# A hybrid decoder layer: a bank of its own for norms, other positions of the mixer's stages, and weight tiles made ahead

## The chip, the cores and the metric

The kernel runs on one NeuronCore of a Trainium2 chip. TensorE (PE) multiplies, and loads its weights in instructions of their own (PEld). VectorE (DVE), ScalarE (ACT) and GpSimd (POOL) do the elementwise work. The queue of SyncE (SP) issues nearly all transfers between DRAM and the on-chip memory. Results of matmuls go to PSUM, eight banks of 512 float32 columns on each of 128 partitions. The metric is the time of the whole program on the device in microseconds; the median of several runs counts.

## The reference

One layer on 512 frames, with 16 meta tokens put ahead of them (528 rows in the kernel, since the pad rows are never computed), model width 1024, all in float32:

```python
h = h + 0.5 * swiglu(rmsnorm(h, norm_ffn1[l]), ffn1_w_in[l], ffn1_w_out[l])
u = rmsnorm(h, norm_mix[l]) * valid
P = u @ w_in[l]
q, kq, vq, rw, gates = jnp.split(P, cols, axis=-1)
...
att = sliding_window_attention(q, kq, vq, sinks[l])
rw = token_shift_lerp(rw, rwkv_mu[l])
r_, k_, v_, wd, ad, gd = jnp.split(rw, rcols, axis=-1)
rwo = rwkv7_time_mix(r_, k_, v_, wd, ad, gd, ...)
g_att, g_rwkv = jnp.split(gates, 2, axis=-1)
merged = (jax.nn.sigmoid(g_att) * (att @ w_attn_branch[l])
          + jax.nn.sigmoid(g_rwkv) * (rwo @ w_rwkv_branch[l]))
h = h + merged @ w_out[l]
h = h + 0.5 * swiglu(rmsnorm(h, norm_ffn2[l]), ffn2_w_in[l], ffn2_w_out[l])
return rmsnorm(h, norm_final)[:, BLOCK:]
```

`swiglu` is `(silu(gate) * up) @ w_out` with 2816 hidden columns. `rwkv7_time_mix` carries a 64 x 64 state for each of 16 heads over all frames: `S = S * w + (S a) b + v k`, `y = S r`.

## The kernel before

**Layout.** Activations lie transposed, eight blocks of 128 features by 528 tokens. Every large product runs in three passes (`products`, L140): each operand is split in a rounded part and the rest (`uh`/`ul`, `whi`/`wlo`), and hi x hi, hi x lo and lo x hi are summed in PSUM. A weight tile of 128 output columns comes in two halves of four feature blocks (256 KB each). `load_w` (L122) loads a half on SyncE's queue into `raw` (three buffers), casts it on ScalarE to `whi` and subtracts on VectorE to get `wlo` (four buffers each).

**Order.** A tile framework puts the instructions in order for every engine by a priority, which is the order in which the program text emits them, and by when it reckons their inputs to be ready. It also sets all waits, among them those on a buffer that is used again. The order on each engine is fixed when the program is built.

**FFN1** (`ffn`, L243). For each of 22 hidden blocks j, the gate's products (`dense`, L258) and then the up products (L261) go to two pairs of banks out of three. The norm is applied behind the product: `nm.end` (L267) sums the squares over features on TensorE (`inverse`, L210), takes the inverse root on VectorE (`rsqrt`) and spreads it over the partitions (L223) into `rstd`; all this uses one bank `pn`. For j = 0 the squares of the first four blocks are made and added on GpSimd (L189 to L194), those of the other four on ScalarE and VectorE. Ahead of it h is loaded in eight pieces, with the four half tiles of j = 0 (both of the gate, both of up) behind pieces 1 and 5. Then eight output blocks, each with its residual addition (L281), its part of the next norm (`tile`, L177) and a store of h.

**Between FFN1 and mixer** (L1089) a new bank `pn` serves `nm.end`, and `scaled` (L226) makes the normalised operand of the mixer. The mixer then takes all eight banks: `dn` 2, `s` 2, `att`, `t`, `y` and `small` 1 each. Its first products, `loras` (L432), and those of `qkv` use the operand that isn't normalised and apply `rstd` later.

**The mixer** (`mixer`, L337) is a set of generators that each `yield` after a step. For each of eight pairs of heads j five stages follow each other: `stage_a1` (projections of k, r, v, the decay, the key norm), `stage_p` (products within chunks of 64 frames, L750), `stage_i` (inverse of the triangular blocks, L839), `stage_b` (the recurrence over nine chunks, L896), `stage_t` (group norm and gate). Beside them run `qkv`, `attend` in eight blocks, 16 `gates` and, at the end, `att_branch`, `reload`, `rwkv_branch`.

`stage_p` clears and fills the blocks `g1` (L767), a ring of two buffers, which `stage_b` reads to its end (L910), and writes the triangular blocks to DRAM (`Ls`, L806). `stage_i` loads them in three copies to `LT` (L847), one buffer, runs 31 steps of a multiplication and an addition on VectorE (L852, L854), writes `Xs` (L858), reads it back to `xt` (L863), and joins the blocks in `assemble` (L870), which uses `LT` as its work space. `stage_b` multiplies by `xt` (L918).

**The planner.** `PLAN` (L40) gives each stage its first position relative to its pair and its span, both in units of one pair; `STEPS` is the number of steps; `SHIFT` moves single stages; `ATTS` and `GATE` are the distances of the attention blocks and gates. `run` (L1002) always emits the step with the lowest position among the stages whose predecessors are done. `LATE` is added to the priority while a step is emitted: a positive number puts its instructions behind others that were emitted later, a negative one ahead.

Of the kernel before, what the change touches and what calls it, by code (L numbers as in the profile page):

```python
# [8 lines left out]
F32 = mybir.dt.float32  # L9
# [30 lines left out]
PLAN = {"qkv": (-3.307, 1), "stage_a1": (-2.9, 1.03), "stage_p": (-1.46, 0.7), "stage_i": (-0.78, 0.75), "stage_b": (-0.201, 0.732),  # L40
        "stage_t": (1.256, 0.532), "att": (-0.985, 0.923), "gate": (-0.058, 1.022), "att_branch": (4.378, 2.027), "reload": (6.272, 0.409), "rwkv_branch": (7.996, 0.282)}
# [57 lines left out]
def hybrid_layer(ctx: ExitStack, tc: tile.TileContext, a, phases="all"):  # L99
# [35 lines left out]
    ready = []  # L135

    def preload(src):
        ready.extend(load_w(src[:, k:k + KW, :], KW) for k in range(0, KD, KW))
# [26 lines left out]
    class Norm:  # L165
# [20 lines left out]
        def square(self, k, h, pool=False):  # L186
            n = self.n
            acc = self.rstd
            if pool:  # L189
                sq = self.tmp.tile([P, NT], F32, name="rms_sq", tag="t")[:, :n] if k else acc[:, :n]  # L190
                nc.gpsimd.tensor_mul(out=sq, in0=h, in1=h)
                if k:
                    nc.gpsimd.tensor_add(out=acc[:, :n], in0=acc[:, :n], in1=sq)
                return  # L194
            if k == 0:
                nc.scalar.activation(out=acc[:, :n], in_=h, func=AF.Square)
            else:
                sq = self.tmp.tile([P, NT], F32, name="rms_sq", tag="t")[:, :n]
                nc.scalar.activation(out=sq, in_=h, func=AF.Square)
                nc.vector.tensor_add(out=acc[:, :n], in0=acc[:, :n], in1=sq)  # L200

        def inverse(self, bank, cols, extra=None):

            n = cols.stop - cols.start
            nb = -(-n // P)
            pt = bank()
            for i, x in enumerate((self.rstd[:, cols], extra)):
                for b in range(nb if x is not None else 0):
                    s0 = min(P * b, n - P)
                    nc.tensor.matmul(pt[:, nb * i + b:nb * i + b + 1], x[:, s0:s0 + P], mean, start=True, stop=True)  # L210
            if extra is None:
                return rsqrt(self.tmp, pt[:, :nb], nb, RMS_EPS)
            ms = self.tmp.tile([P, 8], F32, name="ms")[:, :nb]
            nc.vector.tensor_copy(out=ms, in_=pt[:, :nb])
            nc.vector.tensor_add(out=ms, in0=ms, in1=pt[:, nb:2 * nb])
            return rsqrt(self.tmp, ms, nb, RMS_EPS)
# [26 lines left out]
    def ffn(h, n, nm, w_in, w_out, gain, squares=None):  # L243

        with ExitStack() as es:
# [3 lines left out]
            ps1 = es.enter_context(tc.tile_pool(name="ffn_ps1", bufs=1, space=PSUM))  # L249
            bank = lambda: ps1.tile([P, 512], F32, name="pn")  # L250
# [4 lines left out]
            for j in range(KF):  # L255
                pg = ps2.tile([P, 2, 512], F32, name="dn")
                og, cuts, vg = outs_of(pg, n)
                dense(og, w_in[j, :, 0], nm.uh, nm.ul, KD, cuts)  # L258
                pu = ps2.tile([P, 2, 512], F32, name="dn")
                ou, cuts, vu = outs_of(pu, n)  # L260
                dense(ou, w_in[j, :, 1], nm.uh, nm.ul, KD, cuts)  # L261
# [14 lines left out]
            for i in range(KD - last):  # L276
# [5 lines left out]
                nm.tile(i, h[:, i, :])  # L282
                if gain == "gm":
# [53 lines left out]
    def mixer(nm):  # L337
# [16 lines left out]
        small = ps.tile([P, 512], F32, name="small", bufs=1)  # L354
# [4 lines left out]
        def dense_it(src, cuts, M=P, xh=uh, xl=ul, tags=("dn",), eng=nc.vector):  # L359

            w = []
            for i, c in enumerate(cuts):
                pt = bank(tags[i % len(tags)])[:M, :c.stop - c.start]
                for q in range(KD // KW):
                    if len(w) == q:
                        w.append(load_w(src[:, KW * q:KW * q + KW, :], KW, M, eng))
# [65 lines left out]
        def loras():  # L432
            early = [[x for x in dense_it(w, cuts, M, nm.uh, nm.ul, t) if x[1] is not None]
                     for w, M, cuts, t in ((a["win"][T_LORA], P, HALVES, ("dn",)), (a["win"][T_LORA + 1], P, LATER, ("s",)),
# [32 lines left out]
        def qkv():  # L467
# [6 lines left out]
            for c, pt in dense_it(a["win"][T_VQ], HALVES, P, nm.uh, nm.ul):  # L474
# [592 lines left out]
    with ExitStack() as es:  # L1067
# [21 lines left out]
        with tc.tile_pool(name="nps", bufs=1, space=PSUM) as pn:  # L1089
            nm.tmp = t0  # L1090
            nm.end(lambda: pn.tile([P, 512], F32, name="pn"))
# [3 lines left out]
    with ExitStack() as es:  # L1095
# [110 lines left out]
```

## Time and profile before

| what | us |
|---|---|
| median of 3 runs | 1591.35 |
| lowest, highest run | 1590.21, 1594.18 |
| the profiled execution's own time | 1586.12 |
| its span, first to last instruction | 1584.4 |

By the time line of that execution FFN1 ends at 402.6 us (last product of its last block), the mixer's last result comes at about 1157 us, and the second FFN with its norm fills the rest. Rows of a time line have the start, the time taken, the engine (a q behind it marks the sequencer, which issues and waits), the line of the code, the operation, and the tile that is written and those that are read; xN merges N alike, and in brackets stand the idle time before and what ended it. In a table by stretches each engine has its busy time and its number of instructions. Busy times of PE overlap, as matmuls are pipelined.

### The profile page before, as it was taken

What the parts mean: (1) busy time and instruction counts of PE and PEld (TensorE: products, weight loads), DVE (VectorE), ACT (ScalarE), POOL (GpSimd) and SP (SyncE); (2) the same over time, 40 slices, a digit from 0 to 9 for tenths busy, and PEclk for the clock granted to TensorE, in tenths of its full rate; (3) what the DMA queues carried; (4) which work ended last, traced back from release to release, by engine and by line L of the source; (5) the groups of instructions that cost most, each with busy time, mean ns of one, the idle gap of its engine ahead of it and who ended that gap; (6) DMA issues with size and microseconds to landing.
All of it is one profiled execution on the core that took longest, in us unless ns stands there. A gap on an engine that the chain in (4) does not pass through costs nothing.

```text
span 1584.4 us, 25643 instructions
## 1 busy us (share of the span) xinstructions
PE 1502.9 (95%) x9351; PEld 1322.8 (83%) x9351; DVE 908.3 (57%) x2472; ACT 651.8 (41%) x1464; POOL 103.9 (7%) x159
## 2 busy tenths in 40 slices
PE   7999999999898999999889999979999999999997
PEld 7999999999786887787768788757877888888886
DVE  7434344333745875888888789657555444443334
ACT  4333333232433446474556655644333333333221
POOL 3111111000100100000000000000000011010000
PEclk9999999999899989999999999999999999999998
DMA  5333333333233423133234233347633333333332
GB/s 164 95 89 93 90 91 89 103 110 109 63 111 104 125 72 97 45 96 97 63 102 111 76 96 88 110 147 253 196 104 89 97 94 99 94 98 90 98 91 82
DMA packets 137838, 163.23 MB, mean 103 GB/s; under 512 B 56960, under 2 KB 68288, under 8 KB 137712
## 3 DMA queue, kind: packets, MB, share of 16 engines
q1 hardware_dynamic: 137568, 161.54, 35.0%
q8 instruction: 73, 1.20, 0.3%
q14 instruction: 53, 0.43, 0.1%
q10 hardware_dynamic: 144, 0.06, 0.0%
HBM read 140.03 MB, written 21.52 MB: 102 GB/s over the span
## 4 chain that ended last, share of the span: by engine, by line
PE 77%; DVE 9%; DMA 9%; ACT 3%; issue 2%; SPq 1%; DVEq 0%; ACTq 0%
PE dn L142 17%; PE dn L144 17%; PE dn L143 17%; PE pdn L142 5%; PE pdn L144 4%; PE pdn L143 4%; DMA LT<-Ls 4%; DMA Xs<-X 2%; PE py L923 1%; PE patt L582 1%; DMA raw<-win 1%; PE small L910 1%; DVE wlo L132 1%; PE ps L799 1%; PE small L918 1%
## 5 line engine op out<-in xcount | busy, mean ns | idle before, releaser
L131 ACT CAST whi<-raw 128x512 fp32r<-128x512 f32 (+2 forms) x426 | 259.0, 611 | 594.3 <-PE dn L143 457.7
L132 DVE TENSOR_TENSOR wlo<-raw,whi 128x512 fp32r<-128x512 f32 (+2 forms) x426 | 289.8, 682 | 312.4 <-ACT whi L131 310.9
L142 PE MATMUL dn<-uh,whi 128*128 128x264 f32 (+1 forms) x1320 | 429.5, 326 | 9.1 <-ACT whi L131 6.7
L143 PE MATMUL dn<-ul,whi 128*128 128x264 f32 (+1 forms) x1320 | 427.0, 324 | 1.5 <-DVE ul L181 1.5
L144 PE MATMUL dn<-uh,wlo 128*128 128x264 f32 (+1 forms) x1320 | 427.8, 324 | 0.2 <-DVE wlo L132 0.2
L142 PEld LDWEIGHTS dn<-uh,whi 128*128 128x128 f32 x1320 | 249.5, 189 | 28.8 <-ACT whi L131 9.3
L143 PEld LDWEIGHTS dn<-ul,whi 128*128 128x128 f32 x1320 | 249.8, 189 | 21.9 <-DVE ul L181 2.1
L144 PEld LDWEIGHTS dn<-uh,wlo 128*128 128x128 f32 x1320 | 249.8, 189 | 21.1 <-DVE wlo L132 0.5
L142 PE MATMUL pdn<-uh,whi 128*128 128x264 f32 (+3 forms) x656 | 227.8, 350 | 14.9 <-ACT uh L240 7.4
L144 PE MATMUL pdn<-uh,wlo 128*128 128x264 f32 (+3 forms) x656 | 222.8, 342 | 3.1 <-DVE wlo L132 3.1
L143 PE MATMUL pdn<-ul,whi 128*128 128x264 f32 (+3 forms) x656 | 222.5, 341 | 0.0
L142 PEld LDWEIGHTS pdn<-uh,whi 128*128 128x128 f32 x656 | 127.1, 195 | 29.0 <-ACT uh L240 8.9
L144 PEld LDWEIGHTS pdn<-uh,wlo 128*128 128x128 f32 x656 | 127.1, 194 | 10.7 <-DVE wlo L132 4.6
L143 PEld LDWEIGHTS pdn<-ul,whi 128*128 128x128 f32 x656 | 128.0, 195 | 7.9 <-DVE ul L241 1.5
L143 PE MATMUL dn<-ml,whi 128*128 128x264 f32 (+2 forms) x350 | 110.7, 316 | 0.0
L142 PE MATMUL dn<-mh,whi 128*128 128x264 f32 (+2 forms) x350 | 110.6, 316 | 0.0
L144 PE MATMUL dn<-mh,wlo 128*128 128x264 f32 (+2 forms) x350 | 110.4, 316 | 0.0
L272 POOL TENSOR_TENSOR sg<-sg,rstd 128x528 f32<-128x528 f32 (+1 forms) x44 | 58.0, 1318 | 604.4 <-ACT sg L271 419.0
L273 DVE TENSOR_TENSOR m<-sg,dn 128x528 f32<-128x528 f32 (+1 forms) x44 | 30.6, 696 | 71.0 <-PE dn L144 67.7
L142 PEld LDWEIGHTS dn<-mh,whi 128*128 128x128 f32 x350 | 66.0, 188 | 4.4
L143 PEld LDWEIGHTS dn<-ml,whi 128*128 128x128 f32 x350 | 66.0, 188 | 4.4
L144 PEld LDWEIGHTS dn<-mh,wlo 128*128 128x128 f32 x350 | 66.0, 188 | 4.3
(398 smaller groups left out, 2057.5 us busy)
## 6 DMA issues: line engine op xcount, KB each, us to landing
raw<-win SPq DMA_DIRECT2D x104, 256.0 KB
raw<-w1in SPq DMA_DIRECT2D x88, 256.0 KB
raw<-w2in SPq DMA_DIRECT2D x88, 256.0 KB
raw<-w1out SPq DMA_DIRECT2D x40, 256.0 KB
raw<-w2out SPq DMA_DIRECT2D x40, 256.0 KB
gD<-tgt SPq DMA_DIRECT2D x24, 256.0 KB
raw<-wa SPq DMA_DIRECT2D x16, 256.0 KB
tgt<-gD SPq DMA_DIRECT2D x16, 256.0 KB
```

What stands on the lines that cost most here:

```text
L131: nc.scalar.copy(out=hi, in_=raw)
L132: (eng or nc.vector).tensor_tensor(out=lo, in0=raw, in1=hi.bitcast(F32), op=OP.subtract)
L142: nc.tensor.matmul(o, hi, xh[k][:, c], start=(k == 0), stop=False)
L143: nc.tensor.matmul(o, hi, xl[k][:, c], start=False, stop=False)
L144: nc.tensor.matmul(o, lo, xh[k][:, c], start=False, stop=last)
L272: nc.gpsimd.tensor_mul(out=sg, in0=sg, in1=nm.rstd[:, :n])
L273: nc.vector.tensor_mul(out=vw(m), in0=vw(sg), in1=vu)
L582: nc.tensor.matmul(po[:, x, :], pTs[q][:k1 - k0, P * x:P * x + P], vt[:k1 - k0, q, CH * kv:CH * kv + CH], start=(q == 0), stop=(q == len(p ...
L799: nc.tensor.matmul(pt[:, P * i:P * i + P], KBT[:, c0 + i, :], g1[:, c0 - 1 + i, :], start=True, stop=True)
L910: nc.tensor.matmul(pz[:, U], G.g1[h][:, c - 1, :] if c else G.g0[:, h, :], W[:, c, h, :], start=True, stop=True)
L918: nc.tensor.matmul(pu, G.xt[:, c, :], zy[:, q % 2], start=True, stop=True)
L923: nc.tensor.matmul(py[:, q, h, :], g3[:, c - 1, h, :] if c else G.g3[:, :P], W[:, c, h, :], start=True, stop=True)
```

## The change

- A pool `sm` holds one PSUM bank for the whole program. It serves the norms of both FFNs and the norm between FFN1 and mixer, and it is the mixer's `small`. The extra pools for `pn` go, and behind the mixer three pairs of banks are used instead of four.
- At the start seven products of zeros are run. The half tiles of j = 0 are loaded in another order (first halves of gate and up behind h's piece 0, second halves behind piece 3), and a new `dense_pair` runs gate and up together, block by block of features.
- All squares are made on ScalarE and added on VectorE. `inverse` sums its two parts in PSUM.
- While FFN1 makes its output blocks 2 to 6, one half weight tile of the mixer each is loaded and split into a pool of its own (`FIRST`: both halves of window tiles 0 and 1, the first of tile 27). `dense_it` takes these when it comes to them.
- `PLAN`, `SHIFT`, `ATTS`, `GATE` and `LATE` have other values.

```diff
-PLAN = {"qkv": (-3.307, 1), "stage_a1": (-2.9, 1.03), "stage_p": (-1.46, 0.7), "stage_i": (-0.78, 0.75), "stage_b": (-0.201, 0.732),
-        "stage_t": (1.256, 0.532), "att": (-0.985, 0.923), "gate": (-0.058, 1.022), "att_branch": (4.378, 2.027), "reload": (6.272, 0.409), "rwkv_branch": (7.996, 0.282)}
+PLAN = {"qkv": (-2.771, 0.729), "stage_a1": (-2.83, 0.789), "stage_p": (-1.171, 0.942), "stage_i": (-2.734, 0.587),
+        "stage_b": (-0.138, 0.693), "stage_t": (1.478, 0.214), "att": (-1.614, 1.044), "gate": (0.091, 0.42),
+        "att_branch": (3.86, 1.399), "reload": (6.425, 0.417), "rwkv_branch": (7.903, 0.124)}
...
-SHIFT = {}
-ATTS = 0.971
-GATE = 0.446
-LATE = {"gate": 695, "att_branch": 1783, "reload": 623, "rwkv_branch": 1701, "stage_a1": -77, "stage_t": -265, "stage_p": -66, "stage_i": -182}
+SHIFT = {("stage_t", 5): -0.415, ("stage_i", 7): 0.482, ("stage_b", 2): 0.071, ("stage_a1", 6): -0.027, ("stage_i", 4): -0.133,
...
+        ("stage_t", 7): -0.124, ("stage_t", 1): -0.07, ("stage_i", 0): 0.174, ("stage_p", 5): -0.03, ("stage_b", 7): -0.047}
+
+FIRST = [(0, 0), (0, 1), (1, 0), (1, 1), (27, 0)]
+ATTS = 0.946
+GATE = 0.462
+LATE = {"gate": 337, "att_branch": 1714, "reload": 1055, "rwkv_branch": 2849, "stage_a1": -79, "stage_t": 196, "stage_p": -207,
+        "stage_i": -1108, "qkv": -36, "att": 209, "stage_b": 148}
...
+    sm = ctx.enter_context(tc.tile_pool(name="sm", bufs=1, space=PSUM))
+    bank = lambda: sm.tile([P, 512], F32, name="pn")
     un = ctx.enter_context(ExitStack())
     up = un.enter_context(tc.tile_pool(name="up", bufs=1))
+    pre = un.enter_context(tc.tile_pool(name="pre", bufs=len(FIRST)))
...
+    def dense_pair(outs, src, xh, xl, cuts):
+
+        for k0 in range(0, KD, KW):
+            w = [ready.pop(0) if ready else load_w(src[:, x, k0:k0 + KW, :], KW) for x in range(2)]
+            for k in range(KW):
+                for (hi, lo), oo in zip(w, outs):
+                    for o, c in zip(oo, cuts):
+                        products(o, hi[:, k, :], lo[:, k, :], xh, xl, c, k0 + k, k0 + k == KD - 1)
...
-                            nm.square(k, h[:, k, :], k < 4)
+                            nm.square(k, h[:, k, :])
...
+                if gain == "gm" and i >= 2 and i - 2 < len(FIRST):
+                    t, q = FIRST[i - 2]
+                    first[t, q] = load_w(a["win"][t][:, KW * q:KW * q + KW, :], KW, pool=pre)
...
-        small = ps.tile([P, 512], F32, name="small", bufs=1)
+        small = sm.tile([P, 512], F32, name="pn")
...
+        with tc.tile_pool(name="wps", bufs=1, space=PSUM) as pw:
+            zero, pz = t0.tile([P, 256], F32, name="zero"), pw.tile([P, 512], F32, name="pw")
+            nc.gpsimd.memset(zero, 0.0)
+            for i in range(7):
+                nc.tensor.matmul(pz[:, :256], zero[:, :P], zero, start=True, stop=True)
         for k in range(KD):
             nc.sync.dma_start(out=h[:, k, :], in_=a["xT"][:, k, :])
-            if k in (1, 5) and phases != "mix":
-                preload(a["w1in"][0, :, k // 5])
+            if k in (0, 3) and phases != "mix":
+                preload(a["w1in"][0], KW * (k // 3))
...
-            ps2 = e2.enter_context(tc.tile_pool(name="br_ps", bufs=4, space=PSUM))
+            ps2 = e2.enter_context(tc.tile_pool(name="br_ps", bufs=3, space=PSUM))
```

Left out are the removed GpSimd branch of `square`, the two halves of `inverse` that become one, and the plumbing of `first` through `dense_it`.

More of the change, by code (lines that the diff above doesn't have):

```diff
@@ L39 @@
 PAUSE = {"sq": 1, "rn": 1, "el": 1, "inv": 1}
-PLAN = {"qkv": (-3.307, 1), "stage_a1": (-2.9, 1.03), "stage_p": (-1.46, 0.7), "stage_i": (-0.78, 0.75), "stage_b": (-0.201, 0.732),
-        "stage_t": (1.256, 0.532), "att": (-0.985, 0.923), "gate": (-0.058, 1.022), "att_branch": (4.378, 2.027), "reload": (6.272, 0.409), "rwkv_branch": (7.996, 0.282)}
+PLAN = {"qkv": (-2.771, 0.729), "stage_a1": (-2.83, 0.789), "stage_p": (-1.171, 0.942), "stage_i": (-2.734, 0.587),
+        "stage_b": (-0.138, 0.693), "stage_t": (1.478, 0.214), "att": (-1.614, 1.044), "gate": (0.091, 0.42),
+        "att_branch": (3.86, 1.399), "reload": (6.425, 0.417), "rwkv_branch": (7.903, 0.124)}
 STEPS = {"qkv": 30, "stage_a1": 19, "stage_p": 13, "stage_i": 9, "stage_b": 27, "stage_t": 5, "att": 13, "gate": 2, "att_branch": 24, "reload": 7,
          "rwkv_branch": 16}
-SHIFT = {}
-ATTS = 0.971
-GATE = 0.446
-LATE = {"gate": 695, "att_branch": 1783, "reload": 623, "rwkv_branch": 1701, "stage_a1": -77, "stage_t": -265, "stage_p": -66, "stage_i": -182}
+SHIFT = {("stage_t", 5): -0.415, ("stage_i", 7): 0.482, ("stage_b", 2): 0.071, ("stage_a1", 6): -0.027, ("stage_i", 4): -0.133,
+        ("stage_t", 2): -0.095, ("stage_b", 3): 0.119, ("stage_p", 1): 0.042, ("stage_t", 4): 0.123, ("stage_t", 3): -0.157,
+        ("stage_t", 0): 0.003, ("stage_i", 6): 0.096, ("stage_p", 2): 0.173, ("stage_i", 3): -0.27, ("stage_i", 2): -0.033,
+        ("stage_a1", 3): 0.319, ("stage_p", 6): 0.183, ("stage_a1", 4): 0.07, ("stage_p", 3): -0.095, ("stage_i", 1): 0.055,
+        ("stage_t", 6): -0.097, ("stage_p", 7): 0.076, ("stage_b", 0): 0.067, ("stage_i", 5): -0.243, ("stage_b", 6): 0.153,
+        ("stage_p", 4): 0.028, ("stage_b", 4): -0.102, ("stage_a1", 0): 0.006, ("stage_a1", 2): 0.186, ("stage_b", 1): -0.009,
+        ("stage_t", 7): -0.124, ("stage_t", 1): -0.07, ("stage_i", 0): 0.174, ("stage_p", 5): -0.03, ("stage_b", 7): -0.047}
[4 more added lines that the diff above has]
+        "stage_i": -1108, "qkv": -36, "att": 209, "stage_b": 148}
 S_DECAY = float(np.exp(np.float32(-0.5)))
@@ L133, in load_w, with preload @@
         return hi, lo
-    ready = []
-    def preload(src):
-        ready.extend(load_w(src[:, k:k + KW, :], KW) for k in range(0, KD, KW))
+    ready, first = [], {}
+    def preload(src, k):
+        ready.extend(load_w(src[:, x, k:k + KW, :], KW) for x in range(2))
     def products(o, hi, lo, xh, xl, c, k, last):
@@ L184, in tile, with square @@
                 self.square(k, h)
-        def square(self, k, h, pool=False):
+        def square(self, k, h):
             n = self.n
             acc = self.rstd
[L189 to L194, printed above, removed]
             if k == 0:
@@ L206, in inverse @@
             pt = bank()
[L207 to L216, printed above, removed]
+            for b in range(nb):
+                s0 = min(P * b, n - P)
+                nc.tensor.matmul(pt[:, b:b + 1], self.rstd[:, cols][:, s0:s0 + P], mean, start=True, stop=extra is None)
+                if extra is not None:
+                    nc.tensor.matmul(pt[:, b:b + 1], extra[:, s0:s0 + P], mean, start=False, stop=True)
+            return rsqrt(self.tmp, pt[:, :nb], nb, RMS_EPS)
         def spread(self, bank, y, n):
@@ L365, in dense_it @@
                     if len(w) == q:
-                        w.append(load_w(src[:, KW * q:KW * q + KW, :], KW, M, eng))
+                        ws = a["win"][src] if isinstance(src, int) else src
+                        x = first.pop((src, q), None) if isinstance(src, int) else None
+                        w.append(x or load_w(ws[:, KW * q:KW * q + KW, :], KW, M, eng))
                     for k in range(KW):
@@ L433, in loras @@
             early = [[x for x in dense_it(w, cuts, M, nm.uh, nm.ul, t) if x[1] is not None]
-                     for w, M, cuts, t in ((a["win"][T_LORA], P, HALVES, ("dn",)), (a["win"][T_LORA + 1], P, LATER, ("s",)),
+                     for w, M, cuts, t in ((T_LORA, P, HALVES, ("dn",)), (T_LORA + 1, P, LATER, ("s",)),
                                            (a["wgd"], 32, LATER, ("att", "y")))]
@@ L473, in qkv @@
             vf = T("E2")
-            for c, pt in dense_it(a["win"][T_VQ], HALVES, P, nm.uh, nm.ul):
+            for c, pt in dense_it(T_VQ, HALVES, P, nm.uh, nm.ul):
                 if pt is None:
@@ L1088, in hybrid_layer @@
             return
-        with tc.tile_pool(name="nps", bufs=1, space=PSUM) as pn:
-            nm.tmp = t0
-            nm.end(lambda: pn.tile([P, 512], F32, name="pn"))
+        nm.tmp = t0
+        nm.end(bank)
         nm.scaled(h)
```

9 lines of the change are left out of this document (5 added, 4 removed).

## The prediction

> **What bounds the kernel now.** I read the page first, then stretches of 40 us, then the mixer's periods, then single instructions in order of time.
>
> ```profile
> span 1584.4 us, 25643 instructions
> PE 1502.9 (95%) x9351; PEld 1322.8 (83%) x9351; DVE 908.3 (57%) x2472; ACT 651.8 (41%) x1464; POOL 103.9 (7%) x159
> PE 77%; DVE 9%; DMA 9%; ACT 3%; issue 2%; SPq 1%; DVEq 0%; ACTq 0%
> ```
> ```profile
> 0.00:40.00 40.00, 30.75 (x212) 29.27 (x213) 27.82 (x44) 19.44 (x31) 13.95 (x15) 1.00 0.53 164
> 40.00:80.00 40.00, 40.00 (x331) 40.00 (x330) 16.82 (x25) 13.17 (x21) 3.97 (x3) 1.00 0.33 93
> ```
> The columns of a stretch are PE, PEld, DVE, ACT and POOL busy with their counts, granted clock, DMA share and GB/s. TensorE carries most of the chain, but a busy PE in the table is not a PE at its rate, so I count matmuls. In the settled first FFN there are 331 in 40 us, 0.121 us each. The first 40 us have 212: (331 - 212) x 0.121 = 14.4 us of TensorE are lost at the start. The other stretches of the FFNs read like the second row but for some 1 us, so what can be won lies at the start, between FFN1 and mixer, and in the mixer.
>
> The mixer is a pipeline of eight head pairs j. Here is one whole period and the sum of the seven from 618 to 1063 us (445 / 7 = 63.6 us each), then the instructions on tile X (the elimination of stage_i, L852 and L854) in the same seven:
>
> ```profile
> 680.00:743.00 63.00, 59.94 (x408) 51.37 (x408) 53.10 (x207) 33.51 (x97) 3.64 (x10) 1.00 0.34 100
> sum 445.00, PE 406.56 PEld 341.13 DVE 352.85 ACT 248.61 POOL 22.16; mean PE 58.08 PEld 48.73 DVE 50.41 ACT 35.52 POOL 3.17
> ```
> ```profile
> sum 445.00, DVE 94.94; mean DVE 13.56
> ```
> No engine is full: VectorE works 50.4 of 63.6 us (79%), weight loads 48.7. So a latency sets the period. The SyncE queue, VectorE, TensorE and GpSimd in order of time show which one, for j = 2:
>
> ```profile
> 668.68 0.39 SPq L806 DMA_DIRECT2D Ls<-gg  x1
> 671.99 0.45 SPq L807 DMA_DIRECT2D Ls<-gg  x1
> 678.26 0.89 SPq L847 DMA_DIRECT2D LT<-Ls  x3
> 725.59 4.23 SPq L858 DMA_DIRECT2D Xs<-X  x3
> 734.05 0.30 SPq L863 DMA_DIRECT2D xt<-Xs  x1
> 741.49 0.91 SPq L847 DMA_DIRECT2D LT<-Ls  x3
> ```
> ```profile
> 688.89 0.19 DVE L852 TENSOR_TENSOR xtmp<-LT,X 102x31 f32<-102x31 f32 x1 [1.21 <-DMA LT<-Ls]
> 725.40 0.16 DVE L854 TENSOR_TENSOR X<-X,xtmp 102x11 f32<-102x11 f32 x1
> ```
> ```profile
> 743.58 0.49 PE L918 MATMUL small<-zy,xt 128*128 128x128 f32 x2 [0.82 <-ACT zy L911]
> 776.13 0.43 PE L910 MATMUL small<-W,g1e 128*128 128x64 f32 x2
> ```
> ```profile
> 654.52 0.95 POOL L767 MEMSET g1e<- 64x1024 f32 x1 [0.65 <-PE small L910]
> 776.69 0.95 POOL L767 MEMSET g1e<- 64x1024 f32 x1 [26.36 <-PE small L910]
> ```
> Read as a loop: LT has one buffer, so its load for j = 3 (741.49) goes out when j = 2 is assembled. From load to load 63.2 us pass: 10.6 until the first elimination step, 36.7 of elimination (688.89 to 725.56), 8.5 until xt is fetched, 7.4 of assembly. The recurrence of stage_b can then go on (743.58). A second loop lies around it: stage_p of pair j clears g1e, a ring of two, when stage_b of pair j - 2 has read it last (654.52, 776.69): 122.2 us for two pairs. In it lie 17.9 us of stage_p until Ls is written, 5.8 of waiting for LT, then the 63.2, then 32.6 of stage_b. Of the 36.7 us of elimination only 13.6 are its own work; in the rest VectorE serves other stages between its 62 dependent steps.
>
> **The change part by part.** *Mixer's positions.* Stage_i is placed at -2.734 instead of -0.78 and its priority goes from -182 to -1108. It cannot come before stage_p of its pair, so all its steps stand directly behind it and ahead of what shares VectorE with it. It moves LT, Xs and xt loads on SyncE, its 62 steps on VectorE, one clear on GpSimd (L860) and the assembly on TensorE and ScalarE past stages a1, b and att. At best the elimination falls from 36.7 to 13.6 us and the 5.8 us of waiting go: the two-pair loop becomes 122.2 - 23.1 - 5.8 = 93.3, or 46.7 a pair. Less than VectorE's own 50.4 is not possible. Against it: stage_p's span grows from 0.70 to 0.942 units, and what yields to stage_i is late instead, the copies of stage_b first. I therefore don't take the floor. The best of the periods above kept VectorE at 53.10 / 63 = 84%; that share for all gives 50.4 / 0.843 = 59.8 us, so 3.8 us x 7 periods = 26.6 us, the term I take. Bounds: full VectorE gives 13.2 x 7 = 92 us; from below there is the loss priced with the rivals. The other stages' shifts have no row of their own and are inside these bounds. Gates and attention end earlier (last gate at 7.44 instead of 7.65, last attention step at 6.05 instead of 6.73), which lets the attention branch fill the time of the last recurrence; I count nothing for it.
>
> *FFN1 to mixer.* TensorE and VectorE there:
>
> ```profile
> 402.32 0.28 PE L144 MATMUL dn<-mh,wlo 128*128 128x264 f32 x1
> 406.19 1.50 PE L210 MATMUL pn<-mean,rstd 128*128 128x1 f32 x10 [3.60 <-DVE rstd L200]
> 410.26 2.05 PE L223 MATMUL pn<-con,ny 128*128 128x128 f32 x8 [2.56 <-DVE ny L320]
> 413.09 0.61 PE L223 MATMUL pn<-con,ny 128*128 128x16 f32 x2 [0.78 <-DVE rstd L237]
> 414.06 0.56 PE L142 MATMUL pdn<-uh,whi 128*128 128x264 f32 x1 [0.36 <-DVE rstd L237]
> 414.63 0.42 PE L144 MATMUL pdn<-uh,wlo 128*128 128x264 f32 x1
> 414.85 0.42 PE L142 MATMUL pdn<-uh,whi 128*128 128x264 f32 x1
> 417.41 0.28 PE L142 MATMUL pdn<-uh,whi 128*128 128x264 f32 x1
> 417.53 0.28 PE L143 MATMUL pdn<-ul,whi 128*128 128x264 f32 x1
> ```
> ```profile
> 402.64 0.71 DVE L281 SCALAR_TENSOR_TENSOR h<-dn,h 128x528 f32<-128x528 f32 x1 [0.23 <-PE dn L144]
> ```
> ```profile
> 414.00:440.00 26.00, 25.79 (x201) 25.14 (x202) 23.17 (x43) 17.63 (x32) 0.28 (x3) 0.94 0.19 61
> ```
> The lora products need uh and ul, not the norm, yet the first waits for a copy out of pn: its bank was the norm's. With a bank of its own for the norm they can start after the copy out of dn, at 403.4. Their weights are split in FFN1 in both versions, so only TensorE is asked. The norm's 4.2 us of matmuls (1.50 + 2.05 + 0.61) must be put between. Before, 15 products ran at 0.22 us instead of 0.12 after the pause, 1.5 us. So TensorE is ahead by 414.06 + 1.5 - 403.4 - 4.2 = 8.0 us. The norm's own chain on VectorE stays, so not all comes through. From 414 to 440 us TensorE is busy 25.79 of 26 us and VectorE 23.17: it is nearer to TensorE. Bounds 0 and 8.0, I take 6.
>
> *Five half tiles.* Each costs one 256 KB load on SyncE, one cast on ScalarE and one subtraction on VectorE, put between the loads of w1out. In FFN1 ScalarE works 13.2 of 40 us and VectorE 16.8, TensorE all 40: these hide it, and the ring of weights is free for five more halves. I count nothing; without that cover it would cost five times some 1.3 us.
>
> *Start.*
>
> ```profile
> 6.71 0.59 PE L142 MATMUL dn<-uh,whi 128*128 128x264 f32 x1 [6.71 <-ACT whi L131]
> ```
> ```profile
> 9.61 6.26 DVE L181 SCALAR_TENSOR_TENSOR ul<-h,vec,uh 128x528 fp32r<-128x528 f32 x4 [0.20 <-ACT uh L180]
> 388.07 0.77 DVE L181 SCALAR_TENSOR_TENSOR ul<-h,vec,uh 128x528 fp32r<-128x528 f32 x1 [0.21 <-ACT uh L180]
> 388.75 0.70 DVE L200 TENSOR_TENSOR rstd<-rstd,rms_sq 128x528 f32<-128x528 f32 x1
> ```
> ```profile
> 13.53 3.50 POOL L193 TENSOR_TENSOR rstd<-rstd,rms_sq 128x528 f32<-128x528 f32 x2
> ```
> The gate's and the up weights now both go against each k, so one arrived tile of h gives 12 matmuls instead of 6, and the first weights are loaded one tile earlier. The squares leave GpSimd: beside them four ul took 6.26 us, alone 4 x 0.77 = 3.1, so 3.2 us of VectorE come back, and three more additions (3 x 0.70 = 2.1) take part of it. Of the 14.4 us lost I keep 6 for the first data, and some 3.4 for the cold clock and late tiles: gain 5. Bounds: 14.4 - 6.0 = 8.4, and -2 if the norm, now all on ScalarE and VectorE, holds the banks of the first two results. The seven zero products run before data is there; I give them nothing. The Trainium skill (TensorE: Matmul & The Clock Gate, Part 1: The HAM clock gate) says that the clock is released by a busy window of about 3.4 us that runs freely, and taken back after an idle one: by it the warm-up pays only if it fills such a window and the data follows soon, which would make this term some 2 us larger. No run here shows it yet.
>
> *End.* Two small operations go, on the path behind the last result:
>
> ```profile
> 1573.89 0.16 DVE L214 COPY ms<-pn 128x2 f32<-128x2 f32 x1 [1.15 <-PE pn L210]
> 1574.09 0.16 DVE L215 TENSOR_TENSOR ms<-ms,pn 128x2 f32<-128x2 f32 x1
> ```
> That is 0.4 us. Behind the mixer three pairs of banks instead of four cost nothing: each eviction (0.71 us in the row of L281) is shorter than the 24 products of a tile.
>
> **Sum.** 5 + 6 + 26.6 + 0.4 = 38 us. The profiled execution took 1586.1 us (span 1584.4), the median of the three runs is 1591.35; against the first it gives 1548, against the median 1553. The runs are timed by the median, so I forecast 1553 us.
>
> **The rivals.** *A: the period stays.* The second loop, not the elimination, may set the pace: stage_p is stretched, and each us it loses is lost to the loop. For it: in units the loop is two pairs long in both versions. Against: the 36.7 us with only 13.6 of work. Then 5 + 6 + 0.4 remain: 1580.
>
> *B: slower.* Place: the head of VectorE's queue. The first elimination step waits there for the landing of LT, and now nothing stands before it.
>
> ```profile
> DVE xtmp L852 <- DMA LT<-Ls: 10.2, 5, 3.1
> ```
> Today this is 2.0 us a time, because other work is done in the 10.6 us. If the step is placed right behind its load, VectorE stands 8.6 us more for each of 8 pairs, 69 us, with the copies of stage_b and the emptying of TensorE's banks queued behind it. It decides once more than 11.4 / 8 = 1.4 us of it comes through in each pair. If a third does, 23 us: 1580 + 23 = 1603. Against it: VectorE has 13 us of slack a period.
>
> *C: the loop opens wide.* VectorE reaches the share that TensorE shows, 58.1 / 63.6 = 91%: 50.4 / 0.914 = 55.1, 8.5 x 7 = 59 us; 1591 - 11 - 59 = 1521.
>
> That the norm's bank does not let the loras go first (an order on TensorE that keeps the norm ahead) takes the 6 us away and is inside the forecast.
>
> **How the numbers follow.** Forecast 0.55, A 0.25, B 0.13, C 0.07. With the start and the transition at their bounds the forecast lies from 1548 to 1566; what is unknown is the period. The range, 1525 to 1592, takes in the forecast and A and goes to just short of C at one end and half way from A to B at the other; it leaves out C, the full VectorE behind it, and B, 0.2 together. About 0.3% (4.8 us) can be told from no change here. From A 0.07 and from B 0.01 fall within it. Faster 0.80, same 0.08, slower 0.12.
>
> **What would show it.** Elimination from first to last step under 25 us and periods near 60 us say that the loop was the bound; periods of 63 with a short elimination say A; VectorE waiting over 5 us for LT at each pair says B. Lora products before the norm's matmuls, at the warm rate, show the transition. The first FFN over 4 us earlier shows the start. The forecast is wrong most easily in the share of 84%: one point of it is 0.7 us a period, 5 us in all.

## The result, and the profile after

| | us |
|---|---|
| before, median of 4 runs on the same chip (lowest, highest) | 1590.78 (1585.65, 1594.18) |
| changed kernel, median of 4 runs (lowest, highest) | 1556.27 (1552.94, 1558.12) |
| ratio, 95% interval | 0.9775 (0.9754 to 0.9796) |
| profiled execution of the changed kernel: its time, its span | 1557.82, 1556.1 |

The kernel became 34.5 us faster by the medians and 28.3 us by the spans of the two profiled executions. The head of the changed kernel's page:

```profile
span 1556.1 us, 25641 instructions
PE 1500.3 (96%) x9365; PEld 1325.2 (85%) x9365; DVE 900.1 (58%) x2471; ACT 652.9 (42%) x1468; POOL 93.6 (6%) x153
```

TensorE has the same work and as many busy us; the span is shorter because fewer holes lie between. To find them I cut both executions at the same events of the time line, the starts of single products: the last product of FFN1; the first product of pair 0's recurrence (`py` in `stage_b`); the last product of pair 7's recurrence; then the mixer's last result and the span's end.

| stretch | before, from - to | us | after, from - to | us | difference |
|---|---|---|---|---|---|
| FFN1 | 0 - 402.3 | 402.3 | 0 - 396.6 | 396.6 | -5.7 |
| to the first recurrence | 402.3 - 613.7 | 211.4 | 396.6 - 594.7 | 198.1 | -13.3 |
| first to last recurrence's start | 613.7 - 1058.0 | 444.3 | 594.7 - 1054.2 | 459.5 | +15.2 |
| last recurrence | 1058.0 - 1093.7 | 35.7 | 1054.2 - 1085.2 | 31.0 | -4.7 |
| behind it, to the mixer's end | 1093.7 - 1156.8 | 63.1 | 1085.2 - 1128.8 | 43.6 | -19.5 |
| branch output, FFN2, last norm | 1156.8 - 1584.4 | 427.6 | 1128.8 - 1556.1 | 427.3 | -0.3 |

The surprise stands in the third row: the pipelined periods became no shorter, by these events even longer. What was won lies ahead of them and above all behind them. Here are the busy times of the mixer's stretches (columns as before: PE, PEld, DVE, ACT, POOL, granted clock, DMA share, GB/s), of the kernel before:

```profile
614.00:1058.00 444.00, 406.03 (x2607) 341.51 (x2607) 351.94 (x1371) 247.45 (x724) 22.16 (x56) 0.97 0.33 94
1058.00:1094.00 36.00, 34.46 (x185) 26.92 (x184) 23.21 (x56) 23.35 (x64) 0.00 (x0) 1.00 0.56 183
1094.00:1157.00 63.00, 62.42 (x270) 49.81 (x269) 36.79 (x69) 21.15 (x35) 0.00 (x0) 1.00 0.65 212
```

and of the changed one:

```profile
595.00:1054.00 459.00, 429.98 (x2717) 365.44 (x2717) 363.93 (x1389) 259.23 (x740) 22.27 (x57) 0.96 0.36 104
1054.00:1085.00 31.00, 30.94 (x164) 24.82 (x164) 16.84 (x46) 18.97 (x56) 0.00 (x0) 0.93 0.50 164
1085.00:1129.00 44.00, 43.28 (x188) 34.30 (x187) 29.46 (x59) 16.13 (x28) 0.00 (x0) 1.00 0.64 211
```

The reader is to see two things. Between the first and the last recurrence TensorE does 24.0 us more (429.98 against 406.03) in 15 us more time, so its holes fall from 38.0 to 29.0 us. And behind the last recurrence it is busy without a hole in both kernels: those 63 us were no wait, they were products that hadn't been done earlier, and 82 fewer of them (188 against 270) are left. Which ones, the groups by line tell (count; shortest, median and longest ns; first and last start in us): the gates' tanh, the attention's copy of its result, and the first half of the attention branch's results, before

```profile
L605 ACT ACTIVATE tgt<-pdn x16: 590/597/610, 620.6 to 1037.4; 128x512 f32<-128x512 f32 x16
L593 ACT COPY ao<-patt x16: 366/372/385, 573.3 to 1031.4; 128x256 f32<-128x256 f32 x16
L624 DVE SCALAR_TENSOR_TENSOR tgt<-tgt,pdn x8: 680/686/689, 1064.4 to 1113.6; 128x512 f32<-128x512 f32 x8
```

and after:

```profile
L623 ACT ACTIVATE tgt<-pdn x16: 597/597/617, 589.8 to 1003.0; 128x512 f32<-128x512 f32 x16
L611 ACT COPY ao<-patt x16: 358/372/374, 556.0 to 983.9; 128x256 f32<-128x256 f32 x16
L642 DVE SCALAR_TENSOR_TENSOR tgt<-tgt,pdn x8: 672/684/690, 1026.3 to 1080.2; 128x512 f32<-128x512 f32 x8
```

The last gate comes 34 us and the last attention copy 48 us earlier. The attention branch, which needs both, now gives its results from 1026 to 1080, before the last recurrence ends at 1085; before, they reached 20 us beyond it (1113.6 against 1093.7).

The loop that the prediction meant to shorten, first the seven periods from 599 to 1060 us (461 / 7 = 65.9 us each) and the instructions on tile X in them, then VectorE at the start and the end of pair 2's elimination (L870 and L872 are the old L852 and L854):

```profile
sum 461.00, PE 432.13 PEld 367.18 DVE 363.66 ACT 259.54 POOL 22.17; mean PE 61.73 PEld 52.45 DVE 51.95 ACT 37.08 POOL 3.17
```
```profile
sum 461.00, DVE 93.92; mean DVE 13.42
```
```profile
670.57 0.19 DVE L870 TENSOR_TENSOR xtmp<-LT,X 102x31 f32<-102x31 f32 x1 [1.58 <-DMA LT<-Ls]
670.79 0.29 DVE L951 TENSOR_TENSOR tys<-zy,py 64x128 f32<-64x128 f32 x1
671.12 0.19 DVE L872 TENSOR_TENSOR X<-X,xtmp 102x31 f32<-102x31 f32 x1
671.34 0.28 DVE L951 TENSOR_TENSOR tys<-zy,py 64x128 f32<-64x128 f32 x1
671.54 0.17 DVE L870 TENSOR_TENSOR xtmp<-LT,X 102x30 f32<-102x30 f32 x1
...
706.35 0.16 DVE L872 TENSOR_TENSOR X<-X,xtmp 102x11 f32<-102x11 f32 x1
```

The elimination of pair 2 takes 35.9 us (670.57 to 706.51) where it took 36.7; over the eight pairs the mean is 36.9 us after and 34.6 before. From the start of one elimination to the next (pairs 1 to 7) 65.2 us pass, 64.1 before. Its 62 steps still have 66 to 94 instructions of other stages among them (59 to 96 before): of the 488 gaps between one step and the next, over all pairs, 24 are empty (65 before), although stage_i's priority is now far ahead of theirs.

### The profile page after: what moved, and what is told of

Read it like the earlier page. It is cut to its first block, busy times and chain, and to the rows that moved or that the text cites. A ratio compares the mean times of both kernels' runs of the same rounds, so it can differ in the third digit from the quotient of the medians.

```text
span 1556.1 us, 25641 instructions
## 1 busy us (share of the span) xinstructions
PE 1500.3 (96%) x9365; PEld 1325.2 (85%) x9365; DVE 900.1 (58%) x2471; ACT 652.9 (42%) x1468; POOL 93.6 (6%) x153
## 5 line engine op out<-in xcount | busy, mean ns | idle before, releaser
L144 ACT CAST whi<-raw 128x512 fp32r<-128x512 f32 (+1 forms) x426 | 258.8, 611 | 576.6 <-PE dn L156 446.5
L145 DVE TENSOR_TENSOR wlo<-raw,whi 128x512 fp32r<-128x512 f32 (+1 forms) x426 | 287.9, 679 | 304.1 <-ACT whi L144 300.0
L156 PE MATMUL dn<-ul,whi 128*128 128x264 f32 (+1 forms) x1320 | 427.3, 324 | 0.3 <-DVE ul L203 0.3
```

The costliest lines, as they stand in the source:

```text
L144: nc.scalar.copy(out=hi, in_=raw)
L145: (eng or nc.vector).tensor_tensor(out=lo, in0=raw, in1=hi.bitcast(F32), op=OP.subtract)
L156: nc.tensor.matmul(o, hi, xl[k][:, c], start=False, stop=False)
```

## The experiments

All ratios are against the kernel before, run beside each experiment. Differences to the changed kernel in us are between medians; by the ratios they come out the same within 1 us. A table at the end of this section gives the events of the profiled executions.

**Structure alone**: the changed kernel with the position constants of before.

```diff
-PLAN = {"qkv": (-2.771, 0.729), "stage_a1": (-2.83, 0.789), "stage_p": (-1.171, 0.942), "stage_i": (-2.734, 0.587),
...
+PLAN = {"qkv": (-3.307, 1), "stage_a1": (-2.9, 1.03), "stage_p": (-1.46, 0.7), "stage_i": (-0.78, 0.75), "stage_b": (-0.201, 0.732),
...
+SHIFT = {}
+ATTS = 0.971
+GATE = 0.446
+LATE = {"gate": 695, "att_branch": 1783, "reload": 623, "rwkv_branch": 1701, "stage_a1": -77, "stage_t": -265, "stage_p": -66, "stage_i": -182}
```

> The changed kernel with the position constants of before. Three theories. FILL (attention and gates placed earlier let the attention branch fill holes of the recurrences) and PRIORITY (stage_i's new place and priority) both leave here only the start (5.8 us, the time by which FFN1 ends earlier) and up to 8 us of the transition: 1577 to 1585 us. FRONT (the start and the transition carry the whole gain through the mixer) says 1556 to 1566 us.

Measured: 1575.55 us, ratio 0.9902 (0.9876 to 0.9927). That is 1.5 us below the range of FILL and PRIORITY, and FRONT is out by 10 us. The profiled execution was the slowest of the four (1581.52 us, the others 1573.52 to 1575.61), so its span shows less of the gain than the median does.

**Positions alone**: the kernel before with the constants of the changed one (the last diff turned round; the line `FIRST` comes with them and nothing reads it).

> The kernel before with the position constants of the changed one. FILL and PRIORITY: 34 less 6 to 14 us, so 1563 to 1571 us. FRONT: within 5 us of before, 1586 to 1596 us.

Measured: 1571.59 us, 0.9863 (0.984 to 0.9885), 0.6 us above the range of FILL and PRIORITY; FRONT is out by 14 us. The product of the two ratios, 0.9766, is within the interval of the whole change: the parts add. Of 1591 us the structure brings some 15.6, the positions some 21.8.

**Filling work back**: attention, gates and attention branch at their old positions and priorities, all else as changed.

```diff
-        "stage_b": (-0.138, 0.693), "stage_t": (1.478, 0.214), "att": (-1.614, 1.044), "gate": (0.091, 0.42),
-        "att_branch": (3.86, 1.399), "reload": (6.425, 0.417), "rwkv_branch": (7.903, 0.124)}
+        "stage_b": (-0.138, 0.693), "stage_t": (1.478, 0.214), "att": (-0.985, 0.923), "gate": (-0.058, 1.022),
+        "att_branch": (4.378, 2.027), "reload": (6.425, 0.417), "rwkv_branch": (7.903, 0.124)}
...
+ATTS = 0.971
+GATE = 0.446
+LATE = {"gate": 695, "att_branch": 1783, "reload": 1055, "rwkv_branch": 2849, "stage_a1": -79, "stage_t": 196, "stage_p": -207,
+        "stage_i": -1108, "qkv": -36, "stage_b": 148}
```

> The changed kernel with the positions of attention, gates and attention branch as before. FILL: the 20 us of attention branch fall behind the last recurrence again, 1570 to 1580 us. PRIORITY: unchanged, 1552 to 1560 us.

Measured: 1617.79 us, 1.0159 (1.014 to 1.0178): 61.5 us above the changed kernel. The direction is that of FILL, but the loss is 38 us beyond its range, and larger than all that the positions bring.

**Stage_i back**: its place and its priority as before, and its eight entries in `SHIFT` taken out.

```diff
-PLAN = {"qkv": (-2.771, 0.729), "stage_a1": (-2.83, 0.789), "stage_p": (-1.171, 0.942), "stage_i": (-2.734, 0.587),
+PLAN = {"qkv": (-2.771, 0.729), "stage_a1": (-2.83, 0.789), "stage_p": (-1.171, 0.942), "stage_i": (-0.78, 0.75),
...
-        "stage_i": -1108, "qkv": -36, "att": 209, "stage_b": 148}
+        "stage_i": -182, "qkv": -36, "att": 209, "stage_b": 148}
```

> The changed kernel with stage_i at the position and priority of before. PRIORITY (the forecast's step: 26.6 us of the gain come from stage_i going first): 1575 to 1585 us. FILL: 1552 to 1562 us, as the elimination took some 35 us in both traces.

Measured: 1584.84 us, 0.9955 (0.9939 to 0.9971), 28.6 us above the changed kernel. This is in the range of PRIORITY, and FILL's is missed. So stage_i's place matters among the new positions: with it put back, 68.7 us pass from elimination to elimination instead of 65.2 (pairs 1 to 7). But the elimination that the new place gives (mean 36.9 us instead of 38.9) isn't shorter than before (34.6), and neither is the period (64.1 before).

**No half tiles ahead**:

```diff
-FIRST = [(0, 0), (0, 1), (1, 0), (1, 1), (27, 0)]
+FIRST = []
```

> The changed kernel without the five half tiles made in FFN1 (the mixer loads them itself, through the ring of weights). The forecast counts nothing for them: within 3 us of the changed kernel. The other theory (the time until the first recurrence, 211 us before and 198 after, is shorter because the ring is free for the next weights): 4 to 8 us slower.

Measured: 1561.08 us, 0.9805 (0.9776 to 0.9834). The interval overlaps that of the whole change; the difference of the ratios is 4.8 us, and in the profiled execution the first recurrence starts 5.0 us later. This is nearer to the other theory than to the forecast, without deciding between them.

**Norms in banks of their own pools again**:

```diff
-    sm = ctx.enter_context(tc.tile_pool(name="sm", bufs=1, space=PSUM))
-    bank = lambda: sm.tile([P, 512], F32, name="pn")
+            ps1 = es.enter_context(tc.tile_pool(name="ffn_ps1", bufs=1, space=PSUM))
+            bank = lambda: ps1.tile([P, 512], F32, name="pn")
...
-        small = sm.tile([P, 512], F32, name="pn")
+        small = ps.tile([P, 512], F32, name="small", bufs=1)
...
+        with tc.tile_pool(name="nps", bufs=1, space=PSUM) as pn:
```

> The changed kernel with the norm's banks as before (own pools, so the first lora product waits for the copy out of the norm's bank). The forecast's term: 6 us slower, bounds 0 and 8. The other theory (the mixer's first stages hang on the norm and VectorE): 0 to 2 us slower.

Measured: 1563.31 us, 0.9819 (0.9801 to 0.9837), 7.0 us above the changed kernel; its first recurrence starts 5.6 us later. The forecast's term is borne out.

**No zero products**:

```diff
-            for i in range(7):
-                nc.tensor.matmul(pz[:, :256], zero[:, :P], zero, start=True, stop=True)
```

> The changed kernel without the seven products of zeros. The forecast gives them nothing; from the trace (0.12 us a product from 7.6 us on, where before it was 0.22 us until 17.6) a cold clock for some 3 to 6 us more would cost 2 to 3 us. Theory that they are worth it: 2 to 3 us slower; forecast: within 1 us.

Measured: 1556.87 us, 0.9779 (0.9759 to 0.9799): no difference. The time lines of TensorE, changed kernel and this one, and their stretches from 8 to 10 us:

```profile
1.20 6.23 PE L1096 MATMUL pw<-zero 128*128 128x256 f32 x14 [1.20 <-POOL zero L1094]
7.58 0.36 PE L155 MATMUL dn<-uh,whi 128*128 128x264 f32 x1
```
```profile
6.10 0.59 PE L155 MATMUL dn<-uh,whi 128*128 128x264 f32 x1 [6.10 <-ACT whi L144]
6.48 0.42 PE L156 MATMUL dn<-ul,whi 128*128 128x264 f32 x1
```
```profile
8.00:10.00 2.00, 2.00 (x18) 1.92 (x17) 1.65 (x4) 2.00 (x4) 0.00 (x0) 1.00 0.87 279
```
```profile
8.00:10.00 2.00, 2.00 (x11) 2.00 (x10) 2.00 (x4) 2.00 (x5) 0.00 (x0) 1.00 0.81 188
```

The seven products of zeros stand in the trace as 14 records. With them the first real products run at the warm rate (18 in 2 us instead of 11; the granted clock reads 1.00 in both rows, so the rate is read from the counts), but the zeros themselves hold TensorE until 7.58 us, where data was there at 6.10. The two cancel. The Trainium skill (TensorE: Matmul & The Clock Gate, Part 1: The HAM clock gate) has the clock released after a busy window; the rates agree. The 2 us that the prediction named by it are not there, as the warming products take time from the real ones here.

**Squares on GpSimd again** for the first four blocks:

```diff
-                            nm.square(k, h[:, k, :])
+                            nm.square(k, h[:, k, :], k < 4)
...
+            if pool:
+                nc.gpsimd.tensor_mul(out=sq, in0=h, in1=h)
+                if k:
+                    nc.gpsimd.tensor_add(out=acc[:, :n], in0=acc[:, :n], in1=sq)
```

> The changed kernel with the squares of the first four blocks on GpSimd again. The forecast says that GpSimd slows VectorE at the start (3.2 us for four ul): FFN1 ends 2 to 4 us later and the whole is as much slower. The other theory (TensorE now has 12 products for each arrived block, which hides it): within 1 us.

Measured: 1563.89 us, 0.9823 (0.9807 to 0.984), 7.6 us above the changed kernel, more than the forecast's 2 to 4. The first 40 us of the changed kernel and of this one, then the subtraction `ul` in the first 16 us and the product behind it, in this one:

```profile
0.00:40.00 40.00, 38.31 (x273) 36.18 (x274) 26.19 (x48) 22.26 (x36) 3.53 (x8) 1.00 0.51 162
```
```profile
0.00:40.00 40.00, 35.44 (x237) 33.37 (x238) 28.21 (x43) 19.94 (x31) 14.22 (x15) 0.96 0.46 150
```
```profile
L203 DVE SCALAR_TENSOR_TENSOR ul<-h,vec,uh x3: 1569/1796/1832, 8.9 to 15.3; 128x528 fp32r<-128x528 f32 x3
```
```profile
17.17 0.54 PE L156 MATMUL dn<-ul,whi 128*128 128x264 f32 x1 [3.19 <-DVE ul L203]
```

With GpSimd busy an `ul` takes 1.57 to 1.83 us, in the changed kernel 0.76; TensorE stands for it and is 36 products, 4.4 us, behind at 40 us. FFN1 ends 4.3 us later (400.9); where the rest of the 7.6 us arises isn't known.

**Half of the elimination**:

```diff
-            for c in range(31):
+            for c in range(0, 31, 2):
```

> The changed kernel with every other step of the elimination left out (part of the inverse isn't computed): some 17 us less latency in each pair, and 6.8 us less work on VectorE. LOOP (the forecast's bound: the way from LT to xt sets the period): the two-pair loop falls by 17 us, 8.5 a pair over 7 periods, about 1497 us. FILLED (the period is what VectorE and TensorE need for all that is placed in it, and latency alone is covered): 1526 to 1545 us, of the order of the work that is gone.

Measured: 1557.96 us, 0.9787 (0.9752 to 0.9822), the same as the changed kernel, though the mean elimination fell from 36.9 to 17.2 us (the inverse isn't the right one, as half its steps are left out). LOOP and FILLED both forecast a gain, and neither came. Its stretches:

```profile
584.00:1032.00 448.00, 420.81 (x2695) 362.19 (x2693) 328.76 (x1169) 256.96 (x753) 22.46 (x58) 0.95 0.34 95
1063.00:1133.00 70.00, 69.63 (x302) 55.76 (x300) 40.14 (x73) 23.28 (x39) 0.00 (x0) 1.00 0.69 221
```

The loop hardly became quicker. From the first recurrence's start to the last one's 448.1 us pass instead of 459.5, and from elimination to elimination (pairs 1 to 7) 67.2 instead of 65.2. SyncE shows where the 19.7 us of each pair went, here between pairs 1 and 2:

```profile
618.89 0.33 SPq L881 DMA_DIRECT2D xt<-Xs  x1
...
647.81 0.43 SPq L825 DMA_DIRECT2D Ls<-gg  x1
...
650.32 0.97 SPq L865 DMA_DIRECT2D LT<-Ls  x3
```

In the changed kernel the next load of LT goes out 8.8 us behind that of xt (mean of seven), in five of seven cases 0.1 us behind the last product that reads LT: its one buffer holds it back. Here it goes out 26.6 us behind, LT has then been free for 13 to 23 us in five of seven cases, and the write of `Ls` by stage_p, which it reads, stands 1.8 to 5.4 us ahead of it. So with a short elimination the wait moves to stage_p, and the period stays. The last recurrence ends 22.6 us earlier all the same, 10.5 of which the first one already had; 70 us of products, without a hole, then lie behind it instead of 44, and nothing is won.

**A detour for the inverse**: one more copy in DRAM between `Xs` and `xt`.

```diff
+            Xt = dsc.tile([34, 33, 32], F32, name="Xt")
+            nc.sync.dma_start(out=Xt, in_=Xs)
+            Xs = Xt
```

> The changed kernel with one more copy from DRAM to DRAM (143 KB) between Xs and xt: some 4 to 6 us more latency in each pair and no work for an engine. LOOP: at least half of it in each of 7 periods, 14 to 40 us slower, 1570 to 1596 us. FILLED: within 8 us of the changed kernel.

Measured: 1600.37 us, 1.0056 (1.0033 to 1.0078), 44.1 us above the changed kernel. From elimination to elimination 70.5 us pass instead of 65.2 (starts of pairs 1 and 7: 617.5 and 1040.3 here, 608.3 and 999.2 in the changed kernel; by 6): 5.3 us a pair, eight times 42 us. Of these, 3.0 us lie between the write of Xs and the load of xt (11.5 us instead of 8.5, means of eight) and most of the rest between the load of xt and the next load of LT (11.1 instead of 8.8). The added latency comes through in full and more; how much of it is the place that the extra copy takes in SyncE's queue wasn't separated. It is LOOP's direction, 4 us beyond its range. Behind the last recurrence this time there are holes:

```profile
1129.00:1172.00 43.00, 37.22 (x147) 28.39 (x145) 29.00 (x56) 15.60 (x27) 0.00 (x0) 0.92 0.63 202
```

**The gates alone** at their old place:

```diff
-        "stage_b": (-0.138, 0.693), "stage_t": (1.478, 0.214), "att": (-1.614, 1.044), "gate": (0.091, 0.42),
+        "stage_b": (-0.138, 0.693), "stage_t": (1.478, 0.214), "att": (-1.614, 1.044), "gate": (-0.058, 1.022),
...
-GATE = 0.462
-LATE = {"gate": 337, "att_branch": 1714, "reload": 1055, "rwkv_branch": 2849, "stage_a1": -79, "stage_t": 196, "stage_p": -207,
+GATE = 0.446
+LATE = {"gate": 695, "att_branch": 1714, "reload": 1055, "rwkv_branch": 2849, "stage_a1": -79, "stage_t": 196, "stage_p": -207,
```

> The changed kernel with the 16 gates alone at the positions and the priority of before. The attention branch waits for the last gate. FILL: 8 to 20 us slower, with the products of the attention branch behind the last recurrence again. PRIORITY of stage_i alone: within 4 us.

Measured: 1614.27 us, 1.0141 (1.0106 to 1.0176): 58.0 us above the changed kernel, nearly three times the upper end of what FILL said and nearly all of the third experiment. SyncE of this kernel, then two stretches:

```profile
1047.55 0.34 SPq L881 DMA_DIRECT2D xt<-Xs  x1
...
1067.43 0.34 SPq L998 DMA_DIRECT2D rD<-tys  x1
1069.46 0.34 SPq L1014 DMA_DIRECT2D pT<-rD  x1
1069.84 17.34 SPq L632 DMA_DIRECT2D pT<-aD  x5
```
```profile
1040.00:1060.00 20.00, 8.06 (x30) 6.98 (x30) 1.87 (x6) 4.20 (x17) 0.00 (x0) 0.50 0.11 14
1088.00:1186.00 98.00, 90.36 (x382) 71.92 (x381) 49.65 (x88) 30.09 (x50) 0.00 (x0) 0.97 0.62 197
```

and SyncE of the changed kernel:

```profile
986.34 0.40 SPq L632 DMA_DIRECT2D pT<-aD  x1
...
1048.04 0.33 SPq L881 DMA_DIRECT2D xt<-Xs  x1
```

The load of the attention branch's first operand (`pT<-aD`) is issued at 986 us in the changed kernel, ahead of pair 7's inverse. Here the last gate (1023.8 by its line) is 21 us later, but the load comes 84 us later, because its place in SyncE's queue is now behind the transfers of the last inverse and of the recurrence. TensorE has nothing to fill the last inverse with (8 of 20 us busy, the granted clock at 0.50), and 98 us are left behind the recurrence. The 58 us are the price of the old gates in the new arrangement, not their share of the gain: in the kernel before, with the gates at this same place, the load went out at 1029.9 us.

**Attention alone** at its old place:

```diff
-        "stage_b": (-0.138, 0.693), "stage_t": (1.478, 0.214), "att": (-1.614, 1.044), "gate": (0.091, 0.42),
+        "stage_b": (-0.138, 0.693), "stage_t": (1.478, 0.214), "att": (-0.985, 0.923), "gate": (0.091, 0.42),
...
-ATTS = 0.946
+ATTS = 0.971
...
-        "stage_i": -1108, "qkv": -36, "att": 209, "stage_b": 148}
+        "stage_i": -1108, "qkv": -36, "stage_b": 148}
```

> The changed kernel with attention alone at the positions and the priority of before, its end 0.68 units later. FILL: 10 to 25 us slower, with TensorE idle in the last recurrence and the branch behind it. PRIORITY of stage_i alone: within 4 us.

Measured: 1565.53 us, 0.9836 (0.9808 to 0.9864), 9.3 us above the changed kernel, just under the range of FILL, with the shortest full eliminations of all (mean 34.5 us).

The events of these executions, by their time lines in us; "behind" is from the last recurrence's end to the mixer's end, "elimination" the mean of eight pairs from first to last step:

| kernel | FFN1 ends | first recurrence | last one ends | mixer ends | behind | elimination |
|---|---|---|---|---|---|---|
| before | 402.3 | 613.7 | 1093.7 | 1156.8 | 63.1 | 34.6 |
| changed | 396.6 | 594.7 | 1085.2 | 1128.8 | 43.6 | 36.9 |
| structure alone | 396.1 | 602.7 | 1088.7 | 1151.8 | 63.1 | 34.9 |
| positions alone | 401.8 | 608.1 | 1099.2 | 1142.8 | 43.6 | 37.0 |
| filling work back | 396.1 | 603.3 | 1091.9 | 1189.4 | 97.5 | 35.8 |
| stage_i back | 396.1 | 601.7 | 1110.1 | 1153.9 | 43.8 | 38.9 |
| half the elimination | 396.2 | 584.2 | 1062.6 | 1133.0 | 70.4 | 17.2 |
| detour | 396.4 | 604.4 | 1128.6 | 1172.3 | 43.7 | 37.3 |
| gates alone | 396.1 | 596.0 | 1088.4 | 1185.9 | 97.5 | 34.9 |
| attention alone | 396.0 | 595.0 | 1081.5 | 1136.1 | 54.6 | 34.5 |

These are single executions, and those of one kernel lie up to 16 us apart (no half tiles ahead: 1554.46 to 1570.44), so a difference of a few us between two rows is not firm.

The column "behind" is the key. It is never under 43.6 us, the time that the last recurrence's own branch takes (43.7 to 44.0 in the four executions that the table leaves out); where it is longer, other stages' products have been left over. In those rows the last eight results of the mixer come a steady 5.5 us apart, which is the time of their 24 products (62.42 us / 270 = 0.231 us each, in the stretch behind of the kernel before); in the rows of 44 us they don't. As I read it, the mixer ends 44 us behind the last recurrence, or when TensorE has done all its products, whichever is later. Before, 19.5 us of products were left over. In the changed kernel the two meet: the holes of those 44 us, which the detour's row shows open (37.22 of 43 us busy), are just filled (43.28 of 44). That fits the two experiments on the loop: more latency costs its full price (the detour), less latency wins nothing (half the elimination).

## Why the prediction was right, and where it wasn't

The forecast was 1553 us, the result 1556.27, and it lies in the range. Its reason for the largest term fell all the same; that the total fits so well is in part luck.

- **Start, 5 us taken: right.** FFN1 ends 5.7 us earlier. In the first 40 us there are 273 products, 14 of them of zeros, so 259 of the kernel's own against 212: 47 x 0.121 = 5.7 us. Most of it, 4.4 us, is VectorE freed from GpSimd, as the squares put back show; the step that gave the zero products nothing was right too. The bound of -2 us (the norm holding the banks) didn't come.
- **FFN1 to mixer, 6 us taken: right.** The time line of TensorE after the last product of FFN1, then VectorE's copy that it waits for:

```profile
397.63 0.39 PE L155 MATMUL pdn<-uh,whi 128*128 128x264 f32 x1 [0.80 <-DVE h L294]
...
399.93 1.18 PE L225 MATMUL pn<-mean,rstd 128*128 128x1 f32 x10
...
403.67 1.13 PE L235 MATMUL pn<-con,ny 128*128 128x128 f32 x8 [0.27 <-DVE ny L336]
...
405.62 0.36 PE L235 MATMUL pn<-con,ny 128*128 128x16 f32 x2
```
```profile
396.87 0.71 DVE L294 SCALAR_TENSOR_TENSOR h<-dn,h 128x528 f32<-128x528 f32 x1 [0.23 <-PE dn L157]
```

  The lora products go first, the norm's stand between them, as forecast. Giving the norms their own pools again costs 7.0 us.
- **Five half tiles, nothing taken: a term too small.** They are made without cost in FFN1, but the prediction looked only at what they cost there. It left out what the mixer's first products gain by finding them made: some 5 us, not firmly apart from nothing.
- **Mixer's positions, 26.6 us taken: the size nearly, by luck, the mechanism not.** By the two half-changes it is 19 (from structure alone to the whole) to 22 us (positions alone). The step that failed is "At best the elimination falls from 36.7 to 13.6 us", with the period of 59.8 us that followed. The mean elimination went from 34.6 to 36.9 us and the period from 63.6 to 65.9 (64.1 to 65.2 by the starts of the eliminations). Nor would a shorter elimination alone have shortened it in the changed kernel's order: half the elimination, with a mean of 17.2 us, left it at 67.2. The step that should have carried the term is the one that was counted at nothing, "which lets the attention branch fill the time of the last recurrence". From structure alone to the whole change, by the table of events, the stretch behind the last recurrence loses 19.5 us, the way from FFN1's end to the first recurrence 8.5 (206.6 to 198.1), and the recurrences, which take the work in, grow by 4.5 (486.0 to 490.5). Stage_i's place has its part in this, but not the forecast one: with stage_i back the stretch behind stays at 43.8 us, and the recurrences take 508.4 us (601.7 to 1110.1). It keeps the periods from growing while they take in more work; it doesn't shorten them.
- **What the failed step missed.** I read "No engine is full" and "So a latency sets the period", and stopped at the period. TensorE's 58.08 of 63.6 us (91%) stood in the same row, and the rows behind the periods were in the trace too: from 1094 to 1157 us TensorE was busy 62.42 of 63 us, and until 1113.6 us the attention branch, which comes behind the last gate and the last attention block, was still giving results there. A period is worth shortening only if nothing is left over when the last one ends.
- **Rival A** (the period stays) described the periods nearly and yet gave the wrong time, 1580, because it too priced nothing behind them.
- **Rival B** (VectorE waits for LT) didn't come: the waits of VectorE in the changed kernel

```profile
DVE xtmp L870 <- DMA LT<-Ls: 10.8, 5, 2.8
```

  are 10.8 us in five waits, where they were 10.2 in five: 2.2 us each, not over 5.
- **Rival C** (the loop opens wide) didn't come. **End, 0.4 us:** the stretch behind the mixer is 0.3 us shorter.

What stays open: why the steps of the elimination don't come closer to each other. The rows show one other instruction or more in nearly every gap, whatever the priority; that an uninterrupted block would be better wasn't tried, and half the elimination says that it would win nothing by itself here, with the order of all else as it is. How the positions' gain is shared among the stages isn't known either: the stages put back cost 28.6 to 61.5 us (attention alone 9.3), more than the 19 to 22 us of all positions together, so these are no shares; and neither gates and attention nor stage_i were moved alone in the kernel before. No variant is faster than the changed kernel beyond the noise; without the zero products it is as fast.

## What to carry to other kernels

In a software pipeline look at what is left over when its last loop ends, before shortening the loop: an engine that is busy without a hole there shows work that could have filled earlier holes, and what decides is when the inputs of that work are ready and where its loads stand in their queue. Where loop and filling work end together, as here, less latency in the loop won nothing and more latency cost its full price; whether less would win something with all positions planned anew wasn't tried. And test the reason of a right forecast: here a total that came out 3 us off rested on a mechanism that didn't happen.

## What the runs showed of the hardware that wasn't expected

- Putting one small stage (16 gates) back to its old position cost 58 us in the new arrangement: 21 us of delay of the last gate became 84 us for a load that then stood behind others in SyncE's queue.
- VectorE's subtraction with two operands from the on-chip memory took 1.57 to 1.83 us beside a busy GpSimd and 0.76 alone. The Trainium skill (SBUF — State Buffer, Who interferes with whom) describes such an interference for VectorE instructions with two inputs there beside GpSimd instructions that read there, and calls the shared ports an exclusive lock; that agrees in kind, and the rows here show a bit over a doubling.
- Zero products warm the clock but hold TensorE's queue: 1.5 us later start (7.58 against 6.10) and the warm rate cancel out.
